# One encoder block on eight cores: W_v loaded head by head in turn with the x tiles, V computed in order of arrival, filler matmuls, a respread conv finish and a larger scheduling slack

## The chip, the cores and the metric

The kernel runs on the 8 cores of one Trainium2 chip, two dies of four cores, one batch element per core. The metric is device time in microseconds of the slowest core. In a slow run one die (sometimes both) has a lower granted TensorE clock in the records, and the time is longer.

## The reference

Each core computes one sequence of 2048 tokens, width 2048:

```python
h = rms_norm(x, ln1_g)
u = h @ w_in                        # conv value | conv gate | q | k | v
y_conv = silu(layer_norm(depthwise_conv31(val * sigmoid(gate)) + b_dw))
y_attn = chunked_attention(rms_norm(q), rms_norm(k), v, rel_bias)   # 8 heads of 128
x = x + concat(rms_norm(y_conv), rms_norm(y_attn)) @ w_out
x = x + relu(rms_norm(x) @ w_ff1)**2 @ w_ff2
```

The change touches the beginning (norm of x, and V = h W_v) and the stretch where the conv group is finished (layer norm, silu, gain) while W_out is already multiplied.

## The kernel before

All operations are recorded first; a list scheduler with a simple model of durations then fixes the order of the instructions on each engine. The order is static: at run time an engine waits at its next instruction. `SLACK` is an extra delay that the model assumes between a result of another engine and a TensorE instruction that uses it. It changes no work and no real wait, only the order.

```python
SLACK = 400.0
DMA_BPNS = 310.0
    # schedule(): when operation o on engine e is done, its follower so may start after lat
    lat = 0.0 if (so.eng == e and not o.dma) else XLAT
    ...
    if so.eng == "pe" and e != "pe":
        lat += SLACK
    rt[s] = max(rt[s], o.end + lat)
    # ... among the ready operations of an engine the one earliest in the program is taken
```

The V stage. W_v comes as four blocks of 256 columns (2 MB of float32, cast to bf16 by the transfer), x as 16 tiles of 128 tokens (1 MB). A tile needs all four blocks before the next is begun:

```python
ld = []
for j in range(4):
    ld.append(P.dma("pool", f"wv{j}", wv[:, j, :, :], wv_d[j]))
    if j == 0:
        for t in range(1, 5):
            loadx(t)
...
for t in range(NT):
    norm_tile(...)               # ScalarE square-sum, VectorE scaling, TensorE transposes to hT
    if t + 5 < NT:
        loadx(t + 5)
    for hf in range(4):
        for k in range(16):
            mm(ps(hf, 0, 256), hT[:, qd, k, ...], wv[:, hf, k, :], k == 0, k == 15)
        act(V[:, t, 2*hf:2*hf+2, 0:128], ps(hf, 0, 256)..., AF.Identity)
for j in (1, 2, 3):
    ld[j].deps.add(xo_[2 * j - 1].i)
```

The conv finish. Column group `qd` (512 tokens) is finished channel block by channel block; the first three lines are VectorE and ScalarE work, and TensorE only adds up squares:

```python
def fin_cc(qd, cc):
    stt(yy, yy, pc(bdw2 + cc), ysum[qd][:, :], ALU.add, ALU.subtract)    # VectorE
    tt(yy, yy, rs[:, :], ALU.mult)                                       # VectorE
    act(z, yy, AF.Silu, scale=pc(lng + cc), bias=pc(lnb + cc))           # ScalarE
    P.ts(yb[:, s, qd, 0, :], z, pc(goc + cc), ALU.mult, fast=2.0)        # VectorE
    act(jk, z, AF.Square)                                                # ScalarE
    for j in range(4):
        mm(ps(FB, j, j + 1), jk[128 columns j], onesb[:, 0:1], ...)      # TensorE
# group 0 is finished before W_out starts: fin_cc(0, 0..7), then out_attn(0), conv_dw(6, ..), ...
# c: W_out for the conv half of tile t, a: attention half, s: statistics, f: fin_cc of a group
seq = [("c", 0), ("f", 1, 0, 4), ("a", 2), ("c", 1), ("f", 1, 4, 8), ("c", 2), ("s", 2), ("a", 3), ...]
```

In the feed-forward part, the running sum of a half (8 tiles, `acc`) is loaded two tiles at a time after each of the four W_1 tiles of its first group: `acc_load(2*jj); acc_load(2*jj+1)`.

## Time and profile before

The kernel before takes 2785.49 us (median of 4 runs, 2784.37 to 2788.06).

| stretch (mean of the 8 cores) | us |
|---|---|
| start to the last matmul of the V stage | 181.6 |
| from there to the first W_out matmul (attention, conv) | 549.8 |
| first to last W_out matmul (with the conv finish) | 273.1 |

These are starts of matmuls, read per core from the view of one tile's instructions (`wv`, `wo`). From the page of the kernel before, the span and TensorE's busy time (share of the span, instructions):

```profile
span 2782.1 us, 38484 instructions; the slowest of 8 cores (2778.2 to 2782.1 us)
...
PE 2707.2 (97%) x14445; PEld 1327.1 (48%) x14704; DVE 932.3 (34%) x1482; ACT 830.9 (30%) x1601; POOL 228.1 (8%) x365
```

TensorE is busy 97%, so 75 us is all that is idle. The table of windows of the kernel before says where; the columns are busy us and instruction counts of the engines, then the granted TensorE clock (1.00 is full), the DMA share and GB/s.

```profile
core 0: us, PE busy (x) PEld busy (x) DVE busy (x) ACT busy (x) POOL busy (x), PEclk, DMA share, GB/s
0.00:80.00 80.00, 43.36 (x290) 30.53 (x291) 27.88 (x34) 35.47 (x57) 3.37 (x10) 0.83 0.83 224
690.00:850.00 160.00, 145.41 (x1021) 71.67 (x1038) 123.94 (x163) 91.81 (x126) 35.94 (x35) 0.97 0.58 145
```

The first 80 us hold 36.6 us of idle time and the stretch 690 to 850 us another 14.6. The timeline of TensorE around the conv finish, kernel before, core 0 (start, us, instruction, and in brackets how long TensorE was idle and what released it):

```profile
734.03 2.75 PE L159 MATMUL ps<-wo,yT 128*128 128x512 bf16 x12 [1.49 <-ACT yT L178]
...
740.12 0.24 PE L159 MATMUL ps<-onesb,yb 128*128 128x1 bf16 x4 [1.30 <-ACT yb L178]
...
744.41 2.59 PE L159 MATMUL ps<-wo,yT 128*128 128x512 bf16 x6 [0.84 <-DVE xs_127 L198]
...
768.71 0.38 PE L159 MATMUL ps<-cs,oh 128*4 128x512 bf16 x1 [1.52 <-ACT cs L178]
...
796.69 0.24 PE L159 MATMUL ps<-onesb,jk_125 128*128 128x1 bf16 x4 [1.07 <-ACT jk_125 L178]
...
801.63 2.05 PE L159 MATMUL ps<-ysum_116,onef 128*128 128x512 f32 x2 [1.78 <-ACT rct L178]
```

Until 769 us these are waits around group 0's finish (for `yb` and `xs`; `yT` belongs to the attention half and `cs` to the convolution, which run beside it), at 797 to 802 us waits of group 1 (for the squares `jk`, three times 1.07 to 1.24 us, and the norm `rct`).

### The profile page before, as it was taken

How to read it: one execution, taken by the hardware profiler on the slowest of the kernel's cores; microseconds unless marked ns; L12 is line 12 of the kernel's file. 1: busy time of each engine (PE TensorE's matmuls, PEld its weight loads, DVE VectorE, ACT ScalarE, POOL GpSimd, SP SyncE). 2: the span in 40 equal slices, each digit the busy share in tenths (PEclk: the TensorE clock that was granted, in tenths of full speed). 3: DMA queues.
4: the chain of work that ended last, by engine and by line, in shares of the span. 5: the costliest groups of instructions: out<-in, count | busy, mean ns of one | idle time of the engine just before them, and what ended most of it. 6: DMA issues, size and time to landing. Idle time of an engine off the chain costs nothing.

```text
span 2782.1 us, 38484 instructions; the slowest of 8 cores (2778.2 to 2782.1 us)
## 1 busy us (share of the span) xinstructions
PE 2707.2 (97%) x14445; PEld 1327.1 (48%) x14704; DVE 932.3 (34%) x1482; ACT 830.9 (30%) x1601; POOL 228.1 (8%) x365
## 2 busy tenths in 40 slices
PE   4999999999989999999999999999999999999999
PEld 3875555444444544444444444444444444444444
DVE  3236665655787522022131130220311302202113
ACT  4428887311376431211202102112022021120120
POOL 0000000422500000000000000000000000000000
PEclk8999999999999999999999999999999999999999
DMA  9411110324655478454444444579544444444424
GB/s 243 103 31 36 34 28 11 61 46 76 122 152 167 152 155 177 77 76 76 76 76 76 76 76 76 76 151 196 123 76 76 76 76 76 76 78 76 77 43 137
DMA packets 112455, 256.86 MB, mean 92 GB/s; under 512 B 5393, under 2 KB 83217, under 8 KB 94609
## 3 DMA queue, kind: packets, MB, share of 16 engines
q0 software_dynamic: 92112, 167.82, 37.9%
q1 hardware_dynamic: 20162, 86.56, 9.3%
q8 instruction: 122, 2.00, 0.3%
q14 instruction: 59, 0.48, 0.1%
HBM read 388.60 MB, written 33.55 MB: 152 GB/s over the span
## 4 chain that ended last, share of the span: by engine, by line
PE 94%; DMA 2%; issue 2%; DVE 1%; ACT 1%; ACTq 0%; DVEq 0%; SPq 0%; POOLq 0%
PE ps L159 93%; DMA xa_71<-x 1%; PE ps L163 1%; DMA acc<-out 1%; DMA wc_105<-wcg 0%; DVE y L198 0%; DVE y L192 0%; DVE hb_77 L198 0%; DVE Gt_113 L206 0%; ACT L178 0%; ACT hb_77 L178 0%; DVE hb_78 L198 0%; DVE y L206 0%; DVE yb L203 0%; DVE h2b L198 0%
## 5 line engine op out<-in xcount | busy, mean ns | idle before, releaser
L192 DVE TENSOR_TENSOR acc<-acc,ps 128x512 f32<-128x512 f32 x512 | 351.8, 688 | 1413.3 <-PE ps L159 1401.9
L159 PE MATMUL ps<-yb,fT 128*128 128x512 bf16 x2699 | 596.4, 379 | 4.0 <-DVE acc L192 1.1
L159 PEld LDWEIGHTS ps<-yb,fT 128*128 128x128 bf16 x2752 | 269.1, 98 | 326.3 <-issue 2.1
L178 ACT ACTIVATE rl_134<-ps 128x512 f32<-128x512 f32 x128 | 76.4, 597 | 1102.5 <-PE ps L159 1101.0
L159 PE MATMUL ps<-w2s_138,fT 128*128 128x512 bf16 x1317 | 292.4, 379 | 1.4
L159 PE MATMUL ps<-hTb,yb 128*128 128x512 bf16 x1024 | 242.2, 379 | 0.0
L159 PE MATMUL ps<-yb 128*128 128x512 bf16 x992 | 237.6, 379 | 1.7
L159 PEld LDWEIGHTS ps<-w2s_138,fT 128*128 128x128 bf16 x1344 | 131.5, 98 | 158.6
L225 POOL DMA_DIRECT2D yb<-w x75 | 66.6, 888 | 1173.8 <-PE ps L159 1105.6
L159 PEld LDWEIGHTS ps<-yb 128*128 128x128 bf16 x1024 | 100.2, 98 | 120.8
L159 PEld LDWEIGHTS ps<-hTb,yb 128*128 128x128 bf16 x1024 | 100.2, 98 | 120.3
L178 ACT ACTIVATE rl_135<-ps 128x512 f32<-128x512 f32 x128 | 76.4, 597 | 271.1 <-PE ps L159 271.1
L159 PE MATMUL ps<-wv,hT 128*128 128x256 bf16 x1024 | 120.6, 281 | 5.4 <-DMA wv<-wv 4.0
L159 PE MATMUL ps<-hTb,w1s_136 128*128 128x512 bf16 x512 | 121.0, 379 | 0.0
L159 PE MATMUL ps<-hTb,w1s_137 128*128 128x512 bf16 x512 | 121.0, 379 | 0.0
L159 PE MATMUL ps<-wo,yT 128*128 128x512 bf16 x497 | 117.1, 383 | 3.9 <-ACT yT L178 2.2
L159 PE MATMUL ps<-yb,w1s_136 128*128 128x512 bf16 x480 | 119.3, 379 | 1.7
L159 PE MATMUL ps<-yb,w1s_137 128*128 128x512 bf16 x496 | 117.5, 379 | 0.8
L159 PE MATMUL ps<-hT,wc_105 128*128 128x512 bf16 x498 | 115.0, 381 | 3.4 <-DMA wc_105<-wcg 2.5
L159 PE MATMUL ps<-hT,wc_104 128*128 128x512 bf16 x496 | 117.4, 379 | 0.9
L159 PE MATMUL ps<-wo,yb 128*128 128x512 bf16 x496 | 113.4, 379 | 0.8
L159 PEld LDWEIGHTS ps<-wv,hT 128*128 128x128 bf16 x1024 | 102.6, 101 | 20.6 <-issue 6.3
(300 smaller groups left out, 2741.1 us busy)
## 6 DMA issues: line engine op xcount, KB each, us to landing
yb<-w POOLq DMA_DIRECT2D x75, 1024.0 KB, 10.2
w2s_138<-w POOLq DMA_DIRECT2D x21, 1024.0 KB, 9.5
w1s_136<-w POOLq DMA_DIRECT2D x16, 1024.0 KB, 9.3
w1s_137<-w POOLq DMA_DIRECT2D x16, 1024.0 KB, 9.4
acc<-out SPq DMA_DIRECT2D x16, 1024.0 KB, 11.8
out<-acc SPq DMA_DIRECT2D x64, 256.0 KB, 7.5
wo<-wo POOLq DMA_DIRECT2D x8, 1024.0 KB, 13.4
xs_127<-x SPq DMA_DIRECT2D x6, 1024.0 KB, 6.4
```

The source lines that it names most:

```text
L159: self.op("pe", lambda e: e.matmul(out, lhsT=lhsT, rhs=rhs, start=start, stop=stop, skip_group_check=skip), [lhsT, rhs], [out], f * max(n ...
L163: self.op("pe", lambda e: e.transpose(out, in_, ident), [in_, ident], [out], 64.0)
L178: self.op("act", lambda e: e.activation(out=out, in_=in_, func=func, scale=scale, bias=bias, **kw), r, w, d).func = func
L192: self._ew(eng, lambda e: e.tensor_tensor(out=out, in0=in0, in1=in1, op=op), [in0, in1], [out], fast)
L225: o = self.op(eng, lambda e: e.dma_start(out=out, in_=in_), r, w, 900.0 if eng == "pool" else 350.0, dma=True, key=key, nbytes=nb)
```

## The change

The intent is to keep TensorE fed while x and W_v arrive, and to spread the conv finish evenly over W_out's tiles. The core of the diff:

```diff
-SLACK = 400.0
+SLACK = 700.0
-DMA_BPNS = 310.0
+DMA_BPNS = 320.0
+FILL = 216.0
...
+    def fill_gaps(self, until, reach):       # after scheduling: matmuls of ones in the modelled waits
+        for o in self.order["pe"]:
+            k = max(0, int((o.start - t - SLACK - XLAT) * reach / FILL)) if o.start < until else 0
...
+        self.fill_gaps(60000.0, 0.8)
...
-    wv_d = dr("wv", [4, 128, 16, 256])
+    wv_d = dr("wv", [8, 128, 16, 128])
...
+    chain = [o_gr, xo_[0]]
+    for it in ("w0", "x1", "w1", "x2", "w2", ..., "x7", "w7"):
...
+    for k in range(2, len(chain)):
+        chain[k].deps.add(chain[k - 2].i)     # two loads in flight
...
-        for hf in range(4):
-            ...                               # 256 columns, all blocks, tile after tile
+        for e0, n in VG[min(t, 8)]:           # the heads before head t, in groups of 4, 2, 1
+            vgroup(t, e0, n)
+        if t < 8:
+            for tt_ in range(t + 1):          # head t for all tiles so far
+                vgroup(tt_, t, 1)
...
-    seq = [("c", 0), ("f", 1, 0, 4), ("a", 2), ("c", 1), ("f", 1, 4, 8), ("c", 2), ("s", 2), ("a", 3), ...
+    seq = [("c", 0), ("f", 1, 0, 2), ("a", 2), ("c", 1), ("f", 1, 2, 5), ("c", 2), ("f", 1, 5, 8), ("a", 3), ("c", 3), ("s", 2), ...
```

## The prediction

> **What bounds it now.** TensorE: busy 97% of 2782.1 us on the page, 94% of the chain of waits; 75 us idle. By the table of windows the idle time lies in two places. (a) 0 to 80 us: 36.6 us idle, granted clock 0.81 to 0.84 in most stretches from 20 us and 0.50 from 40 to 50. The DMA share is about 1.0 from 10 to 60 us: TensorE waits for x tiles and W_v, and they stall each other (x tile 5 is 30.29 us of the chain). (b) 720 to 820 us, the conv finish beside W_out: 14.1 us idle, clock 0.88 to 0.95 in three stretches.
>
> **V stage.** Dense from 75.5 us, ends at 182.4 us (first W_qk matmul). By the timeline 64 matmuls of 256 columns take 6.98 us, so 1024 take 112 us; 256 transposes at 56 ns (15 in 0.84 us) take 14 us: about 57 us are lost. The change alternates x tiles and W_v heads (1 MB read each) and makes each pair's work available on arrival. Estimated pace: by 64 us 15.6 MB were written, of which 4.2 MB is cast W_v (read twice as large), so 19.8 MB read in 61 us, 325 GB/s. A pair of 2.1 MB then takes 6.5 us; with one transfer in flight per queue I say 7.3. Tile 0 lands at about 8 us, tile 7 at about 59, and is ready at about 65 (norm chain in the timeline: ACT 2.6, DVE 2.5, transposes and copies 1.5 us). In the changed TensorE order, 34 us of work stand before tile 7's transposes and 93 us after. The 128-column matmuls I take at 56 ns, like the transposes, so finer groups cost nothing. V ends at about 158 us: 24 us gained (16 to 31).
>
> **Fillers.** 33 matmuls of 512 columns, 7 us at full clock, in waits that are there anyway. They keep the clock up (Trainium skill, "TensorE: Matmul & The Clock Gate", Part 1: an idle window of about 3.4 us halves the clock; the clock records agree, 0.5 for 3.4 to 17 us after such gaps). Little work runs there: 1 to 3 us, included in the 24.
>
> **Conv finish.** The crowded second half of column group 1 (793 to 802 us: waits of 0.48 to 1.78 us for h2b, jk, rct) is 6.4 us, plus about 2 us of half clock. Spreading removes most: 6 us. The other 8 us (group 0's finish; waits for yT, yb, cs) keeps its sequence; only the larger scheduling slack can hide it: 3 us.
>
> **Rest.** Attention (99.3% busy) and feed-forward (from 1060 us): unchanged within 2 us; the slack moves order only.
>
> **Prediction.** 24 + 9 + 2 = 35 us less: **2750 us**, 8 times in 10 between 2736 and 2764. Faster by over 2% (under 2730) 0.07; within 2% 0.92; slower 0.01.
>
> **What would show it.** First W_qk matmul near 158 us; TensorE, fillers apart, idle about 25 us in the first 80; no half clock after about 20 us; 128-column V matmuls spaced 56 ns; about 5 us idle in the conv finish instead of 14; everything later shifted as a block.
>
> **What would make it wrong.** One transfer in flight per queue leaving DMA idle (share under 0.9 from 10 to 60 us): pairs of 8.5 us, V ending past 168. Fillers standing before work whose data is there. Weight loads not keeping up at 128 columns (spacing over 70 ns: 9 us or more). More activation table switches making ScalarE the new wait in the finish. The slack opening waits in attention.

## The result, and the profile after

The four runs took 2768.21, 2763.54, 2976.44 and 2969.2 us; the last two are slow (one die at a clock of 0.917), so the median of all, 2868.7 us, is a mixture. The fast runs give a ratio of 0.9928 [0.9904, 0.9952]. (Ratios here are the mean time of one kernel's fast runs over that of the other's fast runs of the same rounds, so not quite the ratio of the medians quoted.) The gain is 19.6 us (the mean of the two fast runs, 2765.9, from 2785.5), not 35. Executions in which one die ran at a lower clock are left out of the means.

| mean of the 8 cores | before | after | predicted change | change |
|---|---|---|---|---|
| V stage ends | 181.6 | 160.3 | -24 | -21.3 |
| from there to the first W_out matmul | 549.8 | 548.3 | } -2 (all the rest) | -1.5 |
| first to last W_out matmul | 273.1 | 271.7 | -9 | -1.4 |
| span of the slowest core (profiled run) | 2782.1 | 2766.7 | -35 | -15.4 |
| mean span of the eight cores | 2780.2 | 2757.3 | | -22.9 |

The view of the cores, profiled run of the changed kernel (span and mean granted clock of each core):

```profile
core 1: 2766.7 us, clock 0.994
...
core 3: 2752.3 us, clock 0.996
```

The spans now lie 14.4 us apart (2752.3 to 2766.7); before it was 4 us (2778.2 to 2782.1).

The page of the changed kernel (span and busy times), then the windows of core 1, its slowest, with the columns as before:

```profile
span 2766.7 us, 38852 instructions; the slowest of 8 cores (2752.3 to 2766.7 us)
...
PE 2723.0 (98%) x14737; PEld 1299.7 (47%) x14737; DVE 932.1 (34%) x1482; ACT 840.0 (30%) x1609; POOL 230.0 (8%) x369
```

```profile
0.00:80.00 80.00, 63.67 (x654) 45.80 (x655) 34.12 (x39) 43.28 (x84) 5.47 (x14) 0.94 0.87 223
690.00:850.00 160.00, 148.09 (x980) 72.14 (x979) 122.74 (x168) 107.58 (x142) 24.72 (x23) 0.96 0.51 145
```

The same table in stretches of 10 us:

```profile
10.00:20.00 10.00, 7.25 (x49) 3.74 (x47) 4.58 (x8) 4.96 (x10) 0.53 (x1) 0.84 0.79 185
20.00:30.00 10.00, 6.82 (x72) 6.20 (x73) 5.38 (x5) 4.42 (x9) 0.53 (x1) 0.67 0.92 231
30.00:40.00 10.00, 8.26 (x106) 6.73 (x104) 3.87 (x4) 5.02 (x9) 1.06 (x2) 1.00 0.83 194
40.00:50.00 10.00, 6.65 (x108) 6.25 (x106) 3.31 (x4) 6.03 (x15) 0.53 (x1) 1.00 0.89 220
50.00:60.00 10.00, 9.89 (x132) 7.86 (x130) 5.71 (x6) 4.96 (x11) 1.06 (x2) 1.00 0.82 241
```

In the first 80 us TensorE is now busy 63.7 us (part of it fillers). The DMA share is 0.79 to 0.92 in these five rows, 0.85 on average: the engines have pauses that the old order did not have (0.98 to 1.01 in the same rows of the kernel before). Core 1 is among the lowest: from 10 to 60 us the mean of the eight cores is 0.92, and 0.93 in the second run of the same kernel (before: 1.01). The clock is 0.84 and 0.67 in the first two rows in spite of the fillers.

The timeline of the V stage on core 1, changed kernel:

```profile
67.25 0.27 PE L188 MATMUL ps<-identb,hb_78 128*128 128x128 bf16 x2
...
71.10 3.73 PE L161 MATMUL ps<-wv,hT 128*128 128x128 bf16 x64 [1.90 <-ACT V L203]
...
155.94 7.07 PE L161 MATMUL ps<-wv,hT 128*128 128x512 bf16 x32
162.84 7.10 PE L161 MATMUL ps<-hT,wqk_66 128*128 128x512 bf16 x32
```

Tile 7's transposes (`hb_78`) start at 67.3 us; 65 was predicted. TensorE does not wait for this tile itself; what delayed it were smaller waits before. The view of the waits, core 1 of the changed kernel (us in total, times, longest), has these lines, all of which lie in the V stage:

```profile
PE ps L161 <- ACT hT L203: 6.9, 4, 2.1
PE ps L161 <- ACT V L203: 3.8, 3, 1.9
...
PE ps L161 <- DMA wv<-wv: 3.1, 2, 1.6
```

64 matmuls of 128 columns, each with its own weight load, take 3.57 us to the next instruction at 74.67, 55.8 ns each, as predicted. The last V matmul starts at 162.6 us.

The same stretch of the conv finish as shown before, changed kernel, core 1:

```profile
710.46 5.34 PE L161 MATMUL ps<-wo,yT 128*128 128x512 bf16 x24 [1.34 <-ACT yT L203]
...
719.63 0.25 PE L161 MATMUL ps<-onesb,yb 128*128 128x1 bf16 x4 [2.13 <-ACT yb L203]
...
722.46 3.57 PE L161 MATMUL ps<-wo,yT 128*128 128x512 bf16 x8 [2.06 <-DVE xs_127 L223]
...
791.66 0.24 PE L161 MATMUL ps<-onesb,jk_125 128*128 128x1 bf16 x4 [1.10 <-ACT jk_125 L203]
793.69 1.23 PE L161 MATMUL ps<-ysum_116,onef 128*128 128x512 f32 x2 [1.79 <-ACT rct L203]
```

Group 1's waits have become fewer (1.10 and 1.79 us are left at 792 to 794 us), but group 0's waits for `yb` and `xs` have grown: 2.13 and 2.06 us where 1.30 and 0.84 stood. TensorE is idle 11.9 us from 690 to 850 us (14.6 before), where about 5 was forecast. The stretch as a whole is only 1.4 us shorter.

The prediction also named a risk: more switches of ScalarE's activation table. They came. From first to last W_out matmul ScalarE loads its table 26 times on core 1 where the kernel before loads it 18 times. The groups of ScalarE of the changed kernel, then of the run with slack 400 (below), whole span:

```profile
L203 ACT ACT_TABLE_LOAD x31 | 39.8, 1283 | 14.9 <-PE ps L161 7.4 <-DVE y L217 3.2 <-DVE rat L237 2.7
L203 ACT ACT_TABLE_LOAD x27 | 34.6, 1283 | 10.7 <-PE ps L161 5.9 <-DVE Gt L231 4.4
```

One load takes 1283 ns, and four of them stand between 780 and 788 us, just before group 1's last waits.

And the wait that makes core 1 the slowest, in its second feed-forward half:

```profile
1951.40 22.23 PE L161 MATMUL ps<-yb,fT 128*128 128x512 bf16 x94 [6.03 <-DVE acc L217]
```

```profile
  DMA acc<-out: 13.2, 3
```

TensorE waits 6.03 us because VectorE cannot add to the running sum: of its idle time before these additions, 13.2 us ended with a load of `acc`. From its last W_out matmul to its end core 1 takes 1784.9 us; cores 0 and 3 take 1775.3. Of these 9.6 us, 7.3 are its three waits for `acc`; the rest fits the clock of 0.92 in the 30 us after 1950 us (an estimate: 30 x 0.08 = 2.4).

### The profile page after: what moved, and what is told of

It is laid out like the page before. It is cut to its first block, busy times and chain, and to the rows that moved or that the text cites. A ratio compares the mean times of both kernels' runs of the same rounds, so it can differ in the third digit from the quotient of the medians.

```text
span 2766.7 us, 38852 instructions; the slowest of 8 cores (2752.3 to 2766.7 us)
## 1 busy us (share of the span) xinstructions
PE 2723.0 (98%) x14737; PEld 1299.7 (47%) x14737; DVE 932.1 (34%) x1482; ACT 840.0 (30%) x1609; POOL 230.0 (8%) x369
## 4 chain that ended last, share of the span: by engine, by line
PE 93%; DMA 4%; ACT 1%; issue 1%; DVE 1%; SPq 0%; ACTq 0%; DVEq 0%; POOLq 0%
PE ps L161 92%; DMA acc<-out 2%; PE ps L188 1%; DMA xa_74<-x 1%; DMA xa_73<-x 1%; DMA xa_71<-x 1%; DMA xa_72<-x 1%; DMA wc_105<-wcg 0%; DMA xa_75<-x 0%; ACT L203 0%; DVE Gt_113 L231 0%; ACT yb L203 0%; DVE y L217 0%; DVE y L223 0%; DVE acc L217 0%
## 5 line engine op out<-in xcount | busy, mean ns | idle before, releaser
L161 PE MATMUL ps<-wv,hT 128*128 128x128 bf16 (+2 forms) x1024 | 117.2, 275 | 14.6 <-ACT hT L203 6.9
L161 PEld LDWEIGHTS ps<-wv,hT 128*128 128x128 bf16 x1024 | 74.7, 99 | 55.1 <-issue 17.6
## 6 DMA issues: line engine op xcount, KB each, us to landing
acc<-out SPq DMA_DIRECT2D x16, 1024.0 KB, 11.9
```

The costliest lines, as they stand in the source:

```text
L161: self.op("pe", lambda e: e.matmul(out, lhsT=lhsT, rhs=rhs, start=start, stop=stop, skip_group_check=skip), [lhsT, rhs], [out], f * max(n ...
```

## The experiments

Stage lengths are means of the eight cores of the profiled run, as in the table above, unless a run's profile is slow. Theories at the start: (1) the V stage works as predicted and its end is set by when tile 7 is ready; (2) the conv finish gained little because group 0's finish is limited by VectorE (it is 99 to 100% busy there); (3) the acc wait is a matter of timing between cores. Rivals are named in the expectations.

### The changed kernel again

No edit.

> The changed kernel once more, as the yardstick for the others of this call. Theory (core-to-core luck in the feed-forward part): fast runs between 2757 and 2770 us, the slowest core set by a wait of some us for the acc loads on one or two cores, not always the same core. Rival (a fixed cost of the change on one core): the same core is slowest with the same 7 us wait as in the first trace.

Measured: 2763.65 us median of four fast runs (2762.4 to 2767.6), ratio 0.9931. V stage 161.0, W_out stretch 272.1. The acc waits of any one core are 2.0 us at most (core 3); core 6 is slowest in the profiled run, core 1 (2766.1) and core 2 (2763.2 and 2760.8) in the others. The slowest core changes: this is luck of timing and no fixed cost of one core. In all six fast runs of the changed kernel its mean is 2764.8.

### Without the fillers

```diff
-        self.fill_gaps(60000.0, 0.8)
```

> The changed kernel without the filler matmuls. Theory (the stage waits for tile 7, fillers only keep the clock up while little work runs): W_v stage ends within 2 us of the changed kernel, time within 3 us, half-clock stretches in the first 70 us as before. Rival (fillers carry the gain): end of the W_v stage 5 us or more later. Other rival (fillers delay work): earlier by 3 us or more.

Measured: V stage ends at 160.4 (160.3 and 161.0 with fillers). The fast runs are 2766.72, 2770.37 and 2767.47, but core 3 has acc waits of 7.4 us in the profiled run, and the mean span of the eight cores, over all fast runs, is 2757.6 (2757.8 with fillers). So the fillers are worth nothing that these runs can show. The clock on core 1 without them:

```profile
10.00:20.00 10.00, 4.43 (x37) 3.47 (x37) 4.91 (x6) 5.02 (x11) 0.53 (x1) 1.00 0.95 228
20.00:30.00 10.00, 8.78 (x113) 8.11 (x111) 5.33 (x6) 4.17 (x9) 1.06 (x2) 1.00 0.93 218
30.00:40.00 10.00, 6.15 (x60) 5.28 (x58) 3.17 (x3) 5.42 (x9) 0.53 (x1) 0.83 1.01 211
```

Its clock is 1.00 where the changed kernel shows 0.84 and 0.67, and 0.83 in the third row, where the changed kernel has 1.00. The page "TensorE: Matmul & The Clock Gate" of the Trainium skill (Part 1) says that idling halves the clock in windows of about 3.4 us and that a busy window restores it; the clocks of these rows fit (0.84 or 0.83 over 10 us is one such window at half clock, 0.67 is two). But the fillers did not shorten the half-clock time: the mean clock of the eight cores over the first 80 us is 0.96 with them (both runs), 0.97 without, and 0.84 in the kernel before. The new order raised it, not the fillers.

### The old finish sequence, slack 700 kept

```diff
-    seq = [("c", 0), ("f", 1, 0, 2), ("a", 2), ("c", 1), ("f", 1, 2, 5), ...
+    seq = [("c", 0), ("f", 1, 0, 4), ("a", 2), ("c", 1), ("f", 1, 4, 8), ...
```

> The changed kernel with the old sequence of the conv finish beside W_out (slack 700 kept). Theory (spreading removes group 1's waits but the slack already hid part of it): stretch from first to last W_out matmul longer by 2 to 5 us than changed. Rival (spreading is worth nothing): within 1 us. My prediction on record: longer by about 6 us.

Measured: W_out stretch 276.9, which is 4.8 us longer than in the run of the changed kernel beside it; time 2769.6 (four fast runs, mean 2770.3; 2764.3 beside it). The spreading is worth about what I predicted (6). But 276.9 is also 3.8 longer than the 273.1 of the kernel before, with the same sequence. What remains is the slack.

### Only finish and slack, V stage untouched

The kernel before with `SLACK = 700.0` and the new `seq`.

> The kernel before with only the new finish sequence and slack 700, W_v stage untouched. Theory (group 0's finish is bound by VectorE, 99 percent busy there, so neither slack nor sequence can help): gain of 1 to 4 us over the kernel before. My prediction on record: gain of about 9 us in this part.

Measured: 2786.51 us, ratio 1.0009 [0.9991, 1.0026]: no gain. The W_out stretch is 271.7, so 1.4 us shorter, and the old V stage ends 3.9 us later (185.5) under the larger slack. My theory's 1 to 4 us were missed, too.

### Slack put back to 400

```diff
-SLACK = 700.0
+SLACK = 400.0
-    (o.start - t - SLACK - XLAT)     # in fill_gaps
+    (o.start - t - 700.0 - XLAT)
```

> The changed kernel with the scheduling slack put back to 400 ns (fillers still counted with 700). Theory A (the larger slack costs in the conv finish, and the new sequence only buys that back): first to last W_out matmul 267 to 269 us instead of 272, time 3 to 6 us below the changed kernel. Rival B (my prediction on record: the slack hides waits): the same stretch longer by 3 us, time above the changed kernel. Rival C: the slack is needed for the W_v stage, its end 3 us or more later.

Measured: W_out stretch 263.6 (262.7 to 264.9 on the cores; 271.0 to 272.7 in the changed kernel). V stage 160.6, unchanged, so rival C falls, and so does B, which was mine. (This is one profile; the two later ones with slack 400 and the new sequence agree.) Only one of four runs was fast, 2760.78, with acc waits of 5.1 and 5.5 us on cores 0 and 3; the mean span of the cores is 2750.5, 6.8 below the changed kernel. The order of VectorE's work shows what is different. First the changed kernel, VectorE's timeline of core 1 in group 0's finish:

```profile
711.64 4.97 DVE L217 TENSOR_TENSOR y<-y,rs 128x512 f32<-128x512 f32 x5
716.53 0.47 DVE L228 TENSOR_SCALAR yb<-y,pv 128x512 bf16<-128x512 f32 x1
```

Then the kernel with slack 400:

```profile
706.60 0.70 DVE L217 TENSOR_TENSOR y<-y,rs 128x512 f32<-128x512 f32 x1
...
709.28 2.34 DVE L217 TENSOR_TENSOR y<-y,rs 128x512 f32<-128x512 f32 x2
711.54 1.26 DVE L228 TENSOR_SCALAR yb<-y,pv 128x512 bf16<-128x512 f32 x1
712.73 0.67 DVE L217 TENSOR_TENSOR y<-y,rs 128x512 f32<-128x512 f32 x1
```

With 700, five multiplications by `rs` stand in a row before the first gain (`yb`, which frees the buffer of the silu and so lets ScalarE go on); with 400, only three come before it, and then gains and multiplications alternate. The first gain starts 6.0 us after the first W_out matmul with 700 and 3.4 us after it with 400. VectorE is equally busy in both (19.9 and 20.0 of the 20 us from 700 to 720). Windows of core 1, changed kernel, then slack 400:

```profile
720.00:740.00 20.00, 16.01 (x104) 7.19 (x105) 11.59 (x18) 10.16 (x16) 3.84 (x5) 0.76 0.29 57
...
780.00:800.00 20.00, 17.11 (x100) 7.95 (x99) 10.39 (x15) 16.26 (x22) 0.89 (x1) 0.91 0.73 191
```

```profile
720.00:740.00 20.00, 18.91 (x155) 9.23 (x154) 14.13 (x18) 6.55 (x10) 9.12 (x8) 0.96 0.18 43
780.00:800.00 20.00, 20.00 (x122) 9.82 (x121) 17.84 (x25) 14.05 (x20) 0.89 (x1) 1.00 0.87 199
```

TensorE is busy 18.9 of 20 us instead of 16.0 in the first of these windows and 20.0 instead of 17.1 in the second, and the clock is 0.96 and 1.00 instead of 0.76 and 0.91: the waits, once long enough, cost clock as well.

### acc loads earlier

```diff
                 if g == 0:
-                    acc_load(2 * jj)
-                    acc_load(2 * jj + 1)
+                    for tt_ in ((0, 1, 2), (3, 4, 5), (6, 7), ())[jj]:
+                        acc_load(tt_)
```

> The changed kernel with the acc loads of each feed-forward half issued after the first, second and third W_1 tile (3, 3 and 2 of them) instead of two after each of four. Theory (the slowest core is set by acc loads landing too late for the first additions): no wait for acc on any core, median 2 to 6 us below the changed kernel, spread of the cores set by the W_v stage alone. Rival (the spread comes only from the W_v stage): no change over 1 us.

Measured: the longest acc wait of any core is 0.3 us; fast runs 2761.38, 2760.93 and 2762.33 (mean 2761.5, against 2764.8 for the changed kernel's six fast runs in other rounds), ratio 0.9919 [0.9901, 0.9937]. So the acc wait costs about 3 us on average (the intervals of the ratios overlap, so this size is not sharp), and up to 9.6 in a single run, as in the first profile. The spans still lie up to 7 us apart (2752.6 to 2759.8): the V stage alone ends 157.1 to 162.3.

### Three loads in flight

```diff
-    for k in range(2, len(chain)):
-        chain[k].deps.add(chain[k - 2].i)
+    for k in range(3, len(chain)):
+        chain[k].deps.add(chain[k - 3].i)
```

> The changed kernel with each load waiting for the load three before it in the chain, not two (three in flight). Theory (with two in flight the DMA engines idle a tenth to a fifth of the time, and tile 7 gates the stage): DMA share over 0.95 from 10 to 60 us, tile 7 ready 3 to 6 us earlier, W_v stage ends 3 to 5 us earlier. Rival (bandwidth bound already): within 1 us. Other rival (order of arrival is spoiled): later.

Measured: V stage ends at 158.0 (160.3 and 161.0), 2 to 3 us earlier; fast runs 2760.1, 2767.67 and 2763.01, so in time it is lost in the scatter of the slowest core. The windows of core 1:

```profile
10.00:20.00 10.00, 7.57 (x41) 3.56 (x39) 3.29 (x4) 3.32 (x7) 0.53 (x1) 0.76 1.00 238
...
30.00:40.00 10.00, 8.19 (x98) 6.45 (x95) 3.88 (x5) 7.49 (x14) 1.06 (x2) 1.00 1.03 235
...
50.00:60.00 10.00, 10.00 (x123) 7.66 (x122) 4.24 (x5) 4.21 (x10) 0.53 (x1) 0.88 0.97 206
```

The DMA share over these five stretches (three are shown) is 0.98 on average instead of 0.85; the mean of the eight cores from 10 to 60 us is 0.98 instead of 0.92. The Trainium skill, "DMA: Bandwidth & Descriptors" (section "Anatomy of one DMA"), gives a fixed cost of about 2.0 us, besides its bytes, to each transfer that GpSimd issues, as it does those of W_v here; the pauses with two in flight, and their end with three, are compatible with this, but no run here measures the 2.0 us.

### Group 0's gains on GpSimd

```diff
-        P.ts(yb[:, s, qd, 0, :], z, pc(goc + cc), ALU.mult, fast=2.0)
+        P.ts(yb[:, s, qd, 0, :], z, pc(goc + cc), ALU.mult, fast=2.0, eng="pool" if qd == 0 else "dve")
```

> The changed kernel with the eight gain multiplications of group 0's conv finish moved from VectorE to GpSimd. Theory (VectorE, 99 to 100 percent busy around group 0's finish, sets its waits): TensorE waits for yb and xs in that stretch (7.6 us in all with yT) fall by 2 to 4 us, time 2 to 4 us lower. Rival (ScalarE or GpSimd slowness sets them): waits the same or longer.

Measured: fast runs 2768.43, 2792.47 and 2769.31 (the second has one die at 2766 to 2791), ratio 0.9974 [0.9923, 1.0024]; W_out stretch 273.6, 1.5 to 1.9 us longer; on core 1 the waits for `yb` are 5.6 us (3.5 in the changed kernel). The groups of GpSimd from 690 to 760 us in this run (busy us, mean ns):

```profile
L228 POOL TENSOR_SCALAR yb<-y,pv 128x512 bf16<-128x512 f32 x8 | 14.4, 1800 | 1.7 <-POOL yb L228 0.8 <-POOL pad L214 0.6 <-PE ps L161 0.2
```

One gain takes 1800 ns here (the slowest core's profile, core 3). On VectorE they take 671 ns on average in the changed kernel, core 1. VectorE was relieved, but each gain became slower, and the waits grew. So the run does not decide whether VectorE's load limits group 0, and theory 2 gets no support from it.

### Slack 400 and earlier acc loads

> The changed kernel with slack 400 and the earlier acc loads, so that the slack can be timed without the acc wait's noise; to be compared with the run of the earlier acc loads alone (2761 to 2762 us). Theory (slack 700 costs about 8 us beside W_out): 2752 to 2756 us. Rival (the one profile with slack 400 was luck): within 2 us of 2761.

Measured: fast runs 2757.3, 2780.23, 2755.81 and 2760.75. The second has two cores at 2775.6 and 2778.7; the ratio with it is 0.9932 [0.9874, 0.9989]. The median of the four is 2759.0. The profile fell in the slow state; on its undisturbed die the W_out stretch is 262.5 to 263.9 us. So the stretch repeats with the slack, and the time is lower than with the earlier loads alone (2761.5), but by less than I expected, and not clearly. The mean span of the eight cores is clearer: 2752.0 in the three undisturbed fast runs, 2756.6 with the earlier loads alone. That is 4.6 us, where the stretch promised 8; the rest is not explained.

### Best version: slack 400, earlier acc loads, three in flight

> The same with three loads in flight instead of two. Theory (adds the 2 to 3 us that the depth gave at the end of the W_v stage): 2750 to 2754 us, lower than both kernels and than the run before it by 1 to 3 us. Rival (depth only adds spread between cores): equal or higher.

Measured: 2754.69, 2751.84, 2756.01 and 2754.71 (mean 2754.3; two more runs slow), ratio 0.9891 [0.9874, 0.9908]. V stage 159.9 (so the third load in flight gives only 0.7 us here, against 160.6 with slack 400 and two), W_out stretch 263.1. It beats both kernels: about 30 us below the kernel before (2784.6 in the same rounds).

### The V part alone

The changed kernel with slack 400 (fillers counted with 700) and the old `seq`.

> The W_v part alone: the changed kernel with slack 400 and the old finish sequence. Theory (parts add up: W_v stage 21 us, old finish with old slack as in the kernel before, 273 us from first to last W_out matmul): 2762 to 2768 us, so the whole of the change's gain, and slack plus sequence together worth nothing on top. Rival (sequence or slack carry part of the gain): 2770 or more.

Measured: 2770.22, 2770.56 and 2770.49, ratio 0.9949. V stage 162.2, W_out stretch 272.1, as the parts add up; but the time reaches the rival's line. In the profiled run core 7, the slowest, has acc waits of 5.7 us; for the other two runs the record has no trace. The mean span of the cores is 2760.5 to 2760.7 in the three runs, 2.8 above the changed kernel's 2757.8 and 19.7 below the kernel before (2780.4). So the V part alone has most of the gain, and slack and sequence together add about 3 us.

### The new loads with the old order of computing

```diff
-        for e0, n in VG[min(t, 8)]:
-            vgroup(t, e0, n)
-        if t < 8:
-            for tt_ in range(t + 1):
-                vgroup(tt_, t, 1)
+        for e0, n in VG[8]:
+            vgroup(t, e0, n)
```

> The new loads (head by head, alternating with x tiles, two in flight) but V computed tile by tile over all heads, as before. Theory (the order of computing makes the gain, the order of loading only permits it): nothing of V can start before the last head lands at 60 to 70 us, the W_v stage ends at 175 to 190 us. Rival (loading order alone gives it): ends at 160 to 165.

Measured: V stage ends at 177.2, time 2781.59 (one run). V does start before the last head, at 33 to 37 us, as soon as the first four heads are there; that detail of the expectation was wrong. Of the 21 us the order of loading alone gives 4.4, the order of computing the other 17. But this run has slack 700, under which the old V stage ends at 185.5 (the run with finish and slack only): against that, the loads (with the fillers) give 8.4. The new order of computing with the old loads was not tried.

### Which engine's order does the slack spoil?

For these three the scheduler runs twice, first with slack 400; the order it gives to one engine is kept, and all the rest is ordered anew with 700:

```diff
-        self.schedule()
+        self.slack = 400.0; self.schedule()
+        pin = [o.i for o in self.order["dve"]]            # or "pe", or "act"
+        # order-only dependencies between neighbours in pin
+        self.slack = 700.0; self.schedule()
+        # and taken out again, so no waits are added
```

> The changed kernel (slack 700, new finish sequence), but VectorE's instructions pinned in the order that slack 400 gives; the other engines are ordered anew with 700 around it. First to last W_out matmul, mean of the eight cores (272 us with 700 throughout, 263.6 with 400). Theory D (the larger slack hurts because it groups VectorE's work, five multiplications by the inverse deviation before the first gain): 264 to 267 us. Rival P (TensorE's own order): 270 to 273. Rival A (ScalarE's order): 270 to 273.

> The same with TensorE pinned in slack 400's order and the others ordered anew with 700. Theory D: 269 to 273 us. Rival P: 264 to 267. Rival A: 269 to 273.

> The same with ScalarE pinned in slack 400's order and the others ordered anew with 700. Theory D: 268 to 273 us. Rival P: 269 to 273. Rival A (order of activations and table loads): 264 to 267.

Measured, W_out stretch: VectorE pinned 262.4, TensorE pinned 274.1, ScalarE pinned 265.6 (271.7 and 272.1 with 700 throughout, 263.6 with 400 throughout). By length alone VectorE's order wins back all of it, ScalarE's 6 us and TensorE's nothing. Rival A's forecast for the pinned ScalarE (264 to 267) came true, theory D's (268 to 273) did not. VectorE's timeline of core 1 with its own order pinned, then with ScalarE's pinned:

```profile
721.82 2.33 DVE L217 TENSOR_TENSOR y<-y,rs 128x512 f32<-128x512 f32 x2
724.08 0.47 DVE L228 TENSOR_SCALAR yb<-y,pv 128x512 bf16<-128x512 f32 x1
```

```profile
727.11 4.98 DVE L217 TENSOR_TENSOR y<-y,rs 128x512 f32<-128x512 f32 x5
732.02 0.47 DVE L228 TENSOR_SCALAR yb<-y,pv 128x512 bf16<-128x512 f32 x1
```

With ScalarE pinned five multiplications still stand before the first gain, and yet the stretch is short. So the five cannot be the whole cause. The table separates the waits of TensorE (0.3 us or more, core 1): group 0 are those for `yb`, `xs` and `yT` from 2 to 25 us after the first W_out matmul, group 1 those for `jk` and `rct`. TensorE executes 1623 or 1624 matmuls in the stretch in all six runs, so no work has moved out of it.

| run | multiplications before the first gain | waits group 0, us | waits group 1, us | ScalarE table loads in the stretch | stretch, us (mean of 8 cores) |
|---|---|---|---|---|---|
| changed (700) | 5 | 5.7 | 2.9 | 26 | 271.7 |
| slack 400 | 3 | 3.4 | 0 | 22 | 263.6 |
| VectorE pinned | 3 | 3.2 | 0 | 22 | 262.4 |
| ScalarE pinned | 5 | 4.9 | 0 | 22 | 265.6 |
| TensorE pinned | 3 | 3.5 | 1.1 | 24 | 274.1 |
| slack 200 (below) | 5 | 7.5 | 0 | 22 | 269.8 |

The slack costs in two places. In group 0 the waits follow VectorE's order: 4.9 to 7.5 us with five multiplications before the first gain, 3.2 to 3.5 with three (3.3 in the kernel before). In group 1 they go with the number of table loads on ScalarE; that the loads cause them is argued, as no run changed them alone. All waits of the stretch together are 11.8 us in the changed kernel and 6.2 with slack 400; the other 2.7 us of the difference on core 1 are not split up, and the lower clock in the windows above is a candidate. The pins do not separate the engines: with TensorE pinned the others, ordered around it, also lose group 0's extra wait, and nothing is won because two waits for `h2b` of 2.6 and 2.7 us appear, which no other run of the table has. So no single engine's order is shown to be the cause.

In time the pins are no improvement (2765.24, 2779.77 and 2773.85, one fast run each): the pinned orders fit the attention stage badly, where from V to W_out 556.2, 551.6 and 562.8 us are needed, not 549.

### Less slack still

The best version with `SLACK = 200.0`.

> The best kernel so far with slack 200. If the cost rises with the slack (each microsecond of slack spreads the chains): first to last W_out matmul at or below 263 us. If 400 is a sweet spot: 265 or more. Attention may lose with less slack: stretch from the end of the W_v stage to the first W_out matmul above 551 us (549 with 400).

Measured: W_out stretch 269.8, V to W_out 551.4, time 2760.32 (one run). So 400 is the best of the three values tried, and the cost does not simply rise with the slack; less is worse too. VectorE again does five multiplications before the first gain, and TensorE then waits 4.4 us for `xs`; group 1 has no waits.

## Why the prediction was right or wrong

The two slack values and the two sequences, W_out stretch in us (means of eight cores):

| | slack 400 | slack 700 |
|---|---|---|
| old sequence | 273.1 (before), 272.1 (V part alone) | 276.9 |
| new sequence | 263.6, 263.1 (best) | 271.7, 272.1 |

- **V stage, 24 us: right.** 21.3 us measured. The mechanism holds: V in order of arrival carries 17 us, the loads 4.4 (8.4 at equal slack). Two to three us are missing: TensorE comes to tile 7 at 67.3 us on core 1, not 65, and the rest takes 95.3 us, not 93, with one more wait of 1.90 us. The loads have a part in it, as two in flight leave the DMA engines idle (share 0.85 on core 1, 0.92 on the mean; I had named this risk with a threshold of 0.9) and three end the stage 2 to 3 us earlier at slack 700; the waits for `hT` and `V` were not tried apart. The 128-column matmuls at 56 ns were right (55.8).
- **Fillers, 1 to 3 us: wrong, small.** Nothing. "No half clock after about 20 us" did not hold on core 1.
- **Spreading of group 1, 6 us: right in mechanism and nearly in size.** 4.8 us at slack 700, and 8.5 at slack 400 (272.1 to 263.6).
- **The step that failed: "only the larger scheduling slack can hide it: 3 us".** The slack was taken as a margin that can only help. It costs 8.3 us in this stretch with the new sequence (263.6 to 271.9, the mean of 271.7 and 272.1) and 3.8 to 4.8 with the old one. It does not act as a delay but as another order: in group 0 five multiplications instead of three come before VectorE's first gain (waits of 5.7 instead of 3.4 us), and in group 1, where 2.9 us of waits remain instead of none, ScalarE switches its table more often (26 loads in the stretch instead of 22), a risk that the prediction had named and not priced. So the conv finish gave 1.4 us and not 9. The 2 us for the rest of the kernel were met (1.5).
- **A term that was missing: the slowest of eight cores.** The sum was made for a typical core, and there the gain is 22.9 us (22.6 over all fast runs with core spans: 2780.4 to 2757.8), but the metric is the slowest core. Over the fast runs the measured time lies 7.0 us above the mean span in the changed kernel, 3.9 in the kernel before, and 4.9 with the earlier acc loads. The spans of the profiled run spread by 14 us because the acc loads came late on one core: 9.6 us on core 1, about 3 us over all fast runs. Why the loads come late on one core and not on another was not tested; that their lateness is the cause of the wait was, as the earlier loads take it away.
- **The sum.** 24 + 9 + 2 = 35 became, on the mean of the cores, 21.3 + 1.4 + 1.5, with the feed-forward part losing 1.2 on average: 22.9 (rounded); and with the slowest core 15 to 20. The fast runs (2763.54 and 2768.21) lie at and above the upper end of my range. The median of all four, 2868.7, is out of it because two runs were slow, of which the prediction says nothing.

Left open: how much VectorE's load, as distinct from its order, limits group 0's finish, and whether ScalarE's table loads cause group 1's waits.

## What to carry to other kernels

A parameter of a scheduler's model is not a safety margin: ask what order it produces on every engine of a chain, not only on the engine that it is meant to protect, and compare two orders before you count it as a gain. Computing in order of arrival, on top of a better order of loading, was worth 17 us here, and the order of loading alone 4 to 8; with transfers of 1 MB two in flight left the DMA engines pauses. When the metric is the slowest of eight cores, a load issued just before its use costs by its worst core, so move it earlier.

## What the Trainium skill lacked or had wrong

- "TensorE: Matmul & The Clock Gate", Part 1, says to budget 13/16 of the clock once three cores of a die run dense matmuls. Here all eight cores run dense matmuls with a granted clock of 1.00 from 2000 to 2100 us and a mean of 0.99 over the run in the fast state. So the condition does not hold here, but the figure does turn up in the slow profile of slack 400 with earlier acc loads: core 4 is at 1.00 until 2100 us and at 0.81 (13/16 is 0.8125) from 2150 to 2860 us, its matmuls of 512 columns 262 ns apart instead of 216. Means such as 0.946 (this core) mix the two.
- The same page, section "Back-to-back issue gap", gives about 81 ns (128 columns) and 131 ns (512) for a sustained stream of weight loads and matmuls. Here 128 columns with a new weight load each are spaced 55.8 ns, and 512 columns 216 ns (32 from 155.94 to 162.84 us on core 1), which are the page's isolated figures.
- "GPSIMD Engine Reference", section 4.1, calls one-input elementwise work roughly line-rate on GpSimd. Here a 128x512 multiplication by a per-partition scalar took 1800 ns there (the profiler's spans on GpSimd are rough) and 671 ns on VectorE (481 ns in the groups after the first).
